# A two-part encoder step on one core: matmul operands at multiples of 512 bytes, small tiles in a pool of their own

## The chip, the cores and the metric

The kernel runs on one core of a Trainium2 chip. The metric is the device time of one execution in microseconds (us), from the first to the last instruction of the core. The kernel before took 1413.92 us (median of three executions: 1413.7, 1413.92 and 1422.26).

The core's engines run side by side and meet at semaphores: PE (matrix multiplications; its weight loads are shown as PEld), DVE (elementwise work, reductions), ACT (elementwise work, exponentials), POOL (elementwise work; it also starts some DMA transfers) and SP (starts most DMA transfers). SBUF is the on-chip memory, PSUM the small one into which PE writes.

## The reference, cut to what matters

All numbers are float32. There are 2048 prompt rows of one stream and 8 x 16 sample rows, which attend to 1024 cached keys each. D is 1024.

```
h = rms_norm(x, norm_g)
z = h @ w_in                                     # 1024 -> 3584 columns
u_a, v_a, g_a, q, k, v, g_b = split(z)           # 7 x 512
# branch A: spatial gate, 4 groups of 128, chunks of 128 positions
vn  = rms_norm(v_a, sgu_norm_g)                  # per group
y_a = u_a * (tril(sgu_w) @ vn + sgu_b) * silu(g_a)
# branch B: differential attention, 4 heads, q and k in two halves of 64
q, k = rms_norm(q, q_norm_g), rms_norm(k, k_norm_g)
s = q.k / 8 - slope_h * |q_pos - k_pos|, block-causal by chunks of 64
o = (softmax(s1) - lam * softmax(s2)) @ v        # lam from four vectors
y_b = rms_norm(o, subln_g) * 0.8 * silu(g_b)     # 0.8 = 1 - lam_init
y = x + concat(y_a, y_b) @ w_out
```

The outputs are y for prompt and sample rows, and the new k, v and v_a. `silu` is computed as 0.5 g (1 + tanh(g/2)), so the tables of `subg` carry the factor 0.5.

## The kernel before, in words

**Arithmetic.** Each float32 operand of a product is split into a high and a low part, both in the fast format `float32r`; `mm3` (L148) then issues three matmuls: high by high, high by low, low by high. A `split` is one ACT copy (the high part) and one subtraction on DVE or POOL (the low part). Most of the 9892 matmuls are such triples: `acc` (projection, 128 x 256), `oo` (output projection, 128 x 512), `oT` (values, 128 x 256). `S` are the scores, and names that end in `_tp` are transposes by the identity `ident`.

**Stages.** There are 17 row tiles of 128 (0 to 15 prompt, 16 the samples). In the profiled execution, whose span is 1410.9 us:

- 0 to about 191 us: the input projection alone (first half of the tiles and the sample rows).
- about 191 to 544 us: the projection woven with the sample attention.
- 544 to about 913 us: the projection of tiles 8 to 15 woven with the prompt attention of query tiles 0 to 7 (four heads, pairs of query tiles); 913 to 942 us: the rest of the projection alone, while the output weights `wo` are loaded and split (L936 to L942).
- 942 to about 1342 us: the output projection woven with the attention of query tiles 8 to 15.
- from about 1342 us: the rest of the output projection with the last values.

**What sets the order.** `weave` (L877) emits two streams of work in turn, by a ratio of their times on PE. When the program is built, a list scheduler then puts the instructions of each engine into one fixed order, by a modelled time line, under the dependencies that tiles and buffers make. On the chip each engine runs its list in that order and only waits for semaphores. In the order of before, the attention of the third stage runs some 1000 emitted instructions behind the place at which `weave` emits it.

**Buffers.** A tile with a tag and `bufs=n` takes the tag's n slots in turn: its first writer waits until the tile that used the slot n allocations earlier has been read for the last time. Two such small tiles matter here:

- `vst` (in `vg_group`, L382 to L403), 2 slots: `va` is copied from the projection's PSUM bank (L392, ACT); ACT squares it and writes sums into `vst` (L400); POOL turns them into factors (L144 to L146); DVE multiplies (`vn`, L403). The PSUM banks of the projection (`acc`, two of them in this stage) come free when `va` and `th` (L367) and their like on ACT and DVE have read them.
- `ost` (in `value_steps`, L629 to L641), 2 slots of its own: the output of a head, `oT`, is copied (`os`, L626), transposed by PE (`o_tp`), squared by ACT with sums into `ost` (L635), POOL makes the factors (L637, L638), and DVE multiplies by the gate (`gbt`, L641).

**Places in memory.** The pools `const`, `const1`, `p1`, `p1g` and `bg` follow each other in SBUF. Small tiles such as `slope` (8 bytes per partition) lie in the same pools as the operands of matmuls, so that the latter start at odd places. By the addresses that the program assigns, modulo 512 bytes: the weights `w` at 448; the transposed rows `xT` of tiles 0 to 3 and 8 to 11 at 128, of tiles 4 to 7 and 12 to 15 at 448, of the samples at 192; `wo` at 480, `yT` at 480 or 192; `kT` and `qT` at 192 or 448; `aT` and `v` of the prompt attention at 128 or 0; `sv` and `saT` of the sample attention at 0.

Of the kernel before, what the change touches and what calls it, by code (L numbers as in the profile page):

```python
# [9 lines left out]
F32 = mybir.dt.float32  # L10
# [3 lines left out]
ALU = mybir.AluOpType  # L14
# [4 lines left out]
P = 128  # L19
# [7 lines left out]
H = 4  # L27
# [5 lines left out]
# buffers  # L33
NEX = (4, 2)        # exponentials of the two softmaxes
NW = 12             # weight chunks
NKB = 6             # chunks of transposed keys
NYT = 2             # halves of a transposed row tile of the output projection
XB = 3              # token tiles on the way in
WB = 5              # weight chunks on the way in, at the start
# what the two streams of a stage get of the tensor engine: the first stream's time over the second's, and how many  # L40
# steps of the second the first may run ahead
RS, AS = 2.8, 100   # projection, sample attention
RA, AA = 2.0, 100   # projection, prompt attention
RB, AB = 0.66, 12   # output projection, prompt attention
RT, AT = 1.8, 0     # output projection, last values
LB = 1.5            # factor on RS for the last sample batch
OB, OT = 9, 6       # time of output projection at the head of its two stages
V0, V1 = 0.25, 1.0  # where in a unit of scores the values of the unit before start and end
QP = 0.3            # and where the queries of the unit after are fetched
CA, CB = "dd", "ad" # engine that scales the second softmax of an even and an odd query tile  # L50
# [7 lines left out]
def trunk_step_kernel(  # L58
# [34 lines left out]

    const = ctx.enter_context(tc.tile_pool(name="const", bufs=1, reuse_waits="tile"))
# [5 lines left out]
    # token tiles: 0..15 prompt, 16 the sample rows  # L100
# [10 lines left out]

    ident = ctile([P, P], "ident")
    mhalf = ctile([P, 8], "mhalf")
    dve.memset(mhalf, -0.5)
    slope = ctile([P, 2], "slope")
    subg = ctile([P, P], "subg")
    neglam = ctile([P, 1], "neglam")

    def constants(lams):
        sp.dma_start(slope, c_slope)  # L120
        sp.dma_start(subg, subln_g[0:1].partition_broadcast(P))
        dve.tensor_scalar_mul(subg, subg, 0.5 * (1.0 - LAM_INIT))
        lame = ctile([P, 2], "lame")
# [34 lines left out]
    def bank(use, name):  # L158
        """The next of the PSUM banks that the stage gives to this use."""
        turn[use] = turn.get(use, -1) + 1  # L160
        b = cur[use][turn[use] % len(cur[use])]
        return psum.tile([P, 512], F32, name=name, tag=f"bank{b}")
# [5 lines left out]
    class Slots:  # L168
        """A pool of equal slots that the streams of a stage share: a tag takes its slots in turn."""
# [17 lines left out]
    def p1_pools(stage, at):  # L187
# [8 lines left out]
        normg = ctile1([P, 8], "normg")  # L196
        qkg = ctile1([P, 2, 2, 64], "qkg")
        sgug = ctile1([P, H, P], "sgug")
        bias_p = ctile1([P, H], "bias_p")
        bias_s = ctile1([P, H], "bias_s")  # L200
        wsT = ctile1([P, 2, H, P], "wsT", F32R)

        def constants1():
            for c in range(2):
                sp.dma_start(qkg[:, 0, c], q_norm_g[0:1].partition_broadcast(P))
                sp.dma_start(qkg[:, 1, c], k_norm_g[0:1].partition_broadcast(P))
# [38 lines left out]
        def xload(t):  # L245
# [9 lines left out]
            st = sb.tile([P, 3], F32, name="xst", tag="xst", bufs=3)  # L255
# [74 lines left out]
        def qk_group(h, tiles, w, loads):  # L330
            for pr, load in zip(pairs(tiles), loads):
# [6 lines left out]
                st = sb.tile([P, 2, 8], F32, name="qst", tag="qst")  # L338
# [7 lines left out]
                pool.tensor_tensor(out=qk[:, :n].rearrange("p n s d -> p n (s d)"),  # L346
                                   in0=z.rearrange("p n s d -> p n (s d)"),
                                   in1=qkg.rearrange("p s c d -> p (s c d)").unsqueeze(1).broadcast_to([P, n, 256]),
                                   op=ALU.mult)
# [32 lines left out]
        def vg_group(h, tiles, w, loads):  # L382
# [5 lines left out]
            for k, (pr, load) in enumerate(zip(pairs(tiles), loads)):  # L388
# [9 lines left out]
                st = sb.tile([P, 2, 2], F32, name="vst", tag="vst")  # L398
# [29 lines left out]
        def stream():  # L428
            """All blocks of columns for the first half of the token tiles and the sample rows, then for the rest."""
# [118 lines left out]
    def score_steps(sl, dist, h, j, ks, qT, wmax, nex, comb, sm):  # L548
        """A step is one chunk of keys for one of the two softmaxes of a query tile."""
        for qi in range(2):  # L550
            t = 2 * j + qi
            w = (t + 1) * P
            st = sl.tile([P, 2, 8], F32, name="sst", tag="sst", bufs=6)
# [38 lines left out]
    def value_steps(sb, vs, h, j, sm):  # L592
# [36 lines left out]
        st = sb.tile([P, 2, 2], F32, name="ost", tag="ost", bufs=2)  # L629
# [17 lines left out]
    def attention(sb, sl, groups, wmax, nk, nv, nex, comb, eng):  # L647
        """A group of pairs of query tiles goes through all heads. The scores of a unit (a pair and a head) run in
        step with the values of the unit before and with the keys and queries of the unit after. Yields None when no
        scores are left."""  # L650
# [28 lines left out]
        for i, (key, j) in enumerate(units):  # L679
            n = size[key[0]]  # L680
            events = []
            # scores
# [5 lines left out]
            # values of the unit before  # L688
# [49 lines left out]
    def sample_scores(sa, b, qkT, qbd, dist_s, res):  # L738
# [8 lines left out]
        st = sa.tile([P, 8], F32, name="sst2", tag="sst2", bufs=2)  # L747
# [56 lines left out]
    def sample_values(sa, b, a):  # L804
# [35 lines left out]
        yield 0  # L840

    def sample_attention(sa):
        """The scores of a batch run in step with the values of the batch before."""
        ss = sample_setup(sa)
        yield pe_time(1024)
        a = None
# [220 lines left out]
```

## Time and profile before

| | before |
|---|---|
| median of three executions | 1413.92 us |
| profiled execution: own time, first to last instruction (span) | 1410.9 us |
| PE busy | 1360.5 us (96%), 9892 matmuls |
| DVE busy | 897.1 us (64%) |
| ACT busy | 794.0 us (56%) |
| POOL busy | 617.6 us (44%) |
| mean granted PE clock | 0.994 |

The profiled execution's own time is its span; nothing is added around it. A line such as L73 is the line of a helper (`mm3`), so groups are told apart by their tiles: `acc<-w,xT` is the projection. A matmul's duration in the records (284 ns for `acc`) is longer than the distance from one start to the next, because matmuls overlap in the array; distances are read from the timeline, where a row gives the time from the first start to the last end of n matmuls in a row.

### The profile page before, as it was taken

To read this page: it belongs to the slowest core of one execution; us is meant where nothing else is said; L and a number is where in the kernel's file an instruction comes from. 1 tells how busy PE (TensorE), PEld (TensorE's weight loads), DVE (VectorE), ACT (ScalarE), POOL (GpSimd) and SP (SyncE) were. 2 spreads that over 40 slices of the span, in tenths; PEclk is the share of its full clock that TensorE was granted. 3 is DMA by queue.
4 is the path that set the end of the run, shared out by engine and by line. 5 is a ranking of instruction groups with operands and counts; after the bars stand their busy time and mean duration, and the time that the engine had idled before them with its cause. 6 is when DMAs were issued, how large, how long until landed. Compare 5 with 4: busy or idle time off the path is not lost.

```text
span 1410.9 us, 27990 instructions
## 1 busy us (share of the span) xinstructions
PE 1360.5 (96%) x9892; PEld 1266.1 (90%) x9892; DVE 897.1 (64%) x2114; ACT 794.0 (56%) x1778; POOL 617.6 (44%) x796
## 2 busy tenths in 40 slices
PE   7999999999999989899999999988999999999998
PEld 6999999999999979899999999986888888888887
DVE  5442366767565764786766767444888778878632
ACT  5442356666655775565554655443777767667520
POOL 2361535555554655656232331243555545444310
PEclk9999999999999999999999999998999999999999
DMA  7533244545444476445343332166555433433223
GB/s 220 175 91 100 78 122 124 169 130 158 130 140 145 142 220 203 112 112 138 96 128 83 99 96 69 42 211 207 149 158 162 142 115 117 143 97 94 75 94 101
DMA packets 209245, 183.06 MB, mean 130 GB/s; under 512 B 21104, under 2 KB 167024, under 8 KB 209104
## 3 DMA queue, kind: packets, MB, share of 16 engines
q1 hardware_dynamic: 199280, 155.17, 36.9%
q0 software_dynamic: 9824, 26.09, 6.8%
q8 instruction: 78, 1.28, 0.4%
q14 instruction: 63, 0.52, 0.1%
HBM read 130.86 MB, written 42.47 MB: 123 GB/s over the span
## 4 chain that ended last, share of the span: by engine, by line
PE 50%; DMA 7%; DVE 5%; ACT 3%; issue 3%; POOL 3%; SPq 1%; ACTq 0%; DVEq 0%; POOLq 0%
PE acc L73 16%; PE oo L73 12%; PE S L73 8%; PE oT L73 7%; PE a_tp L77 4%; DMA wraw<-in_w_in_dram 2%; DMA svraw<-in_cache_v_dram 1%; DMA woraw<-in_w_out_dram 1%; DVE ex L584 1%; DMA x<-in_x_prompt_dram 1%; DVE ex L568 1%; PE y_tp L77 1%; DMA qraw<-q_scr 1%; POOL sv L139 1%; DVE w L306 1%
## 5 line engine op out<-in xcount | busy, mean ns | idle before, releaser
L73 PE MATMUL acc<-w,xT 128*128 128x256 f32 x5376 | 719.4, 284 | 2.5 <-DVE w L306 0.9
L73 PEld LDWEIGHTS acc<-w,xT 128*128 128x128 f32 x5376 | 676.2, 190 | 14.8 <-issue 2.7
L73 PE MATMUL oo<-wo,yT 128*128 128x512 f32 x816 | 223.6, 405 | 6.6 <-ACT yT L138 6.6
L73 PE MATMUL S<-kT,qT 128*128 128x512 f32 (+3 forms) x688 | 185.8, 367 | 6.2 <-DVE sst L568 3.9
L572 ACT ACTIVATE ex<-ex,sst 128x128 f32<-128x128 f32 (+15 forms) x128 | 153.9, 1203 | 61.0 <-DVE sst L568 59.5
L73 PEld LDWEIGHTS oo<-wo,yT 128*128 128x128 f32 x816 | 148.9, 191 | 34.7 <-ACT yT L138 7.6
L306 DVE SCALAR_TENSOR_TENSOR w<-wraw,normg,w 128x256 fp32r<-128x256 f32 x224 | 119.6, 555 | 87.1 <-ACT w L305 79.1
L305 ACT ACTIVATE w<-wraw,normg 128x256 fp32r<-128x256 f32 x220 | 105.8, 505 | 87.8 <-DMA wraw<-in_w_in_dram 75.3
L73 PE MATMUL oT<-aT,v 128*128 128x256 f32 x864 | 151.8, 290 | 2.9 <-ACT aT L138 1.9
L568 DVE CUSTOM_DVE_ANT_0 ex<-S,dist,sst 128x512 f32<-128x512 f32 (+2 forms) x192 | 123.2, 652 | 37.6 <-PE S L73 35.8
L73 PEld LDWEIGHTS oT<-aT,v 128*128 128x128 f32 x864 | 124.3, 189 | 14.5 <-DVE aT L139 3.9
L139 POOL TENSOR_TENSOR sv<-svraw,sv 128x512 fp32r<-128x512 f32 (+1 forms) x72 | 96.6, 1346 | 75.5 <-ACT sv L138 59.1
L73 PEld LDWEIGHTS S<-kT,qT 128*128 128x128 f32 x688 | 110.4, 191 | 21.3 <-DVE sst L568 8.6
L138 ACT CAST aT<-a_tp 128x512 fp32r<-128x512 f32 (+1 forms) x144 | 79.3, 559 | 70.4 <-PE a_tp L77 68.5
L139 DVE TENSOR_TENSOR aT<-a_tp,aT 128x512 fp32r<-128x512 f32 (+1 forms) x144 | 94.3, 658 | 38.2 <-ACT aT L138 37.3
L568 DVE CUSTOM_DVE_ANT_0 ex<-S,dist 128x512 f32<-128x512 f32 (+3 forms) x128 | 79.6, 629 | 29.8 <-PE S L73 16.6
L77 PE MATMUL a_tp<-ident,ex 128*128 128x128 f32 x544 | 83.1, 273 | 4.3 <-DVE ex L584 3.3
L784 POOL TENSOR_TENSOR slo<-slo,dist_s 64x256 f32<-64x256 f32 (+1 forms) x64 | 49.4, 772 | 63.3 <-ACT slo L783 60.5
L139 POOL TENSOR_TENSOR v<-vraw,v 128x512 fp32r<-128x512 f32 x36 | 48.2, 1338 | 54.5 <-ACT v L138 45.4
L77 PEld LDWEIGHTS a_tp<-ident,ex 128*128 128x128 f32 x544 | 63.3, 140 | 8.5 <-DVE gbt L641 1.9
L584 DVE SCALAR_TENSOR_TENSOR ex<-ex,sst 128x1024 f32<-128x1024 f32 (+4 forms) x64 | 65.1, 1038 | 1.1
L588 POOL TENSOR_TENSOR ex<-ex 128x1024 f32<-128x1024 f32 (+4 forms) x32 | 58.4, 1848 | 15.9 <-ACT ex L587 11.4
(144 smaller groups left out, 1925.5 us busy)
## 6 DMA issues: line engine op xcount, KB each, us to landing
wraw<-in_w_in_dram SPq DMA_DIRECT2D x160, 128.0 KB, 2.5
skraw<-in_cache_k_dram SPq DMA_DIRECT2D x64, 256.0 KB, 3.1
svraw<-in_cache_v_dram SPq DMA_DIRECT2D x64, 256.0 KB, 2.9
kT<-k_scr POOLq DMA_DIRECT2D x20, 512.0 KB, 4.6
vraw<-out_dram SPq DMA_DIRECT2D x36, 256.0 KB, 2.8
y<-y_scr SPq DMA_DIRECT2D x34, 256.0 KB, 3.0
out_dram<-xo SPq DMA_DIRECT2D x34, 256.0 KB, 2.1
wraw<-in_w_in_dram SPq DMA_DIRECT2D x128, 64.0 KB, 2.2
```

Source lines behind the costliest of these rows:

```text
L73: pe.last = nc.tensor.matmul(*a, **k).ins
L77: pe.last = nc.tensor.transpose(*a, **k).ins
L138: act.copy(hi, src)
L139: (lo_eng or dve).tensor_tensor(out=lo, in0=src, in1=f(hi), op=ALU.subtract)
L305: act.activation(w[:, 0], r, AF.Copy, scale=normg[:, kc:kc + 1])
L306: dve.scalar_tensor_tensor(out=w[:, 1], in0=r, scalar=normg[:, kc:kc + 1], in1=f(w[:, 0]), op0=ALU.mult, op1=ALU.subtract)
L568: dve.tensor_tensor_reduce(out=ex[c][:, a:b], in0=s, in1=dist[:, off + a:off + b], scale=SLOPES[h], scalar=prev[c], op0=ALU.add, op1=ALU.m ...
L572: act.activation(ex[c][:, :w], ex[c][:, :w], AF.Exp, bias=prev[c], scale=-1.0, accum_out=st[:, c, 6:7])
L584: dve.scalar_tensor_tensor(out=p0, in0=p1, scalar=st[:, 1, 7:8], in1=p0, op0=ALU.mult, op1=ALU.add)
L588: pool.tensor_tensor(out=p0, in0=p1, in1=p0, op=ALU.add)
L784: pool.tensor_tensor(out=lo, in0=lo, in1=dist_s[rh, x:x + w_], op=ALU.add)
```

## The change

1. A new pool `small` at the bottom of SBUF takes all small tiles: the constants as slices of one tile `misc`, and the tags `xst`, `qst`, `sst`, `sst2`, `vst`. `ost` is now allocated under the tag `vst`, so that `vg_group` and `value_steps` take turns in one ring of 3 slots. `sfst` shares `sst2`.
2. The table `qkg` of query and key norms is halved ([P, 2, 64], read twice by a broadcast). Two DMA loads go. The multiplication on POOL (L346), 32 times 128 x 512, becomes two of 128 x 256 each.
3. `subg` moves to `const1`.
4. The pool `bg` is preceded by a pad of 120 columns, and its slots of odd sizes are allocated first. Which slots hold what in the prompt attention of the third stage changes (`qT` in m10 and m0, `eb` in m11).
5. With this, the operands that the front part lists by address all start at multiples of 512 bytes (`w`, `xT`, `wo`, `yT`, `kT`, `qT`, `aT`, `v`, `vhl`, `wsT`, `ident`); only some inputs of transposes and the key slices of the sample scores start elsewhere.

```diff
+    small = ctx.enter_context(tc.tile_pool(name="small", bufs=2, reuse_waits="tile"))
     const = ctx.enter_context(tc.tile_pool(name="const", bufs=1, reuse_waits="tile"))
...
+    misc = small.tile([P, 32], F32, name="misc", tag="misc", bufs=1)
+    mhalf, normg, slope, neglam, lame = [misc[:, a:b] for a, b in ((0, 8), (8, 16), (16, 18), (18, 19), (19, 21))]
+    bias_p, bias_s = misc[:, 21:25], misc[:, 25:29]
+    dve.memset(mhalf, -0.5)
     ident = ctile([P, P], "ident")
-    mhalf = ctile([P, 8], "mhalf")
-    dve.memset(mhalf, -0.5)
-    slope = ctile([P, 2], "slope")
-    subg = ctile([P, P], "subg")
-    neglam = ctile([P, 1], "neglam")
...
-        qkg = ctile1([P, 2, 2, 64], "qkg")
+        subg = ctile1([P, P], "subg")
+        qkg = ctile1([P, 2, 64], "qkg")
...
-            st = sb.tile([P, 3], F32, name="xst", tag="xst", bufs=3)
+            st = small.tile([P, 3], F32, name="xst", tag="xst", bufs=3)
...
-                pool.tensor_tensor(out=qk[:, :n].rearrange("p n s d -> p n (s d)"),
-                                   in0=z.rearrange("p n s d -> p n (s d)"),
-                                   in1=qkg.rearrange("p s c d -> p (s c d)").unsqueeze(1).broadcast_to([P, n, 256]),
-                                   op=ALU.mult)
+                for i in range(n):
+                    pool.tensor_tensor(out=qk[:, i].rearrange("p s (c d) -> p s c d", c=2),
+                                       in0=z[:, i].rearrange("p s (c d) -> p s c d", c=2),
+                                       in1=qkg.unsqueeze(2).broadcast_to([P, 2, 2, 64]), op=ALU.mult)
...
-                st = sb.tile([P, 2, 2], F32, name="vst", tag="vst")
+                st = small.tile([P, 2, 2], F32, name="vst", tag="vst", bufs=3)
...
-            st = sl.tile([P, 2, 8], F32, name="sst", tag="sst", bufs=6)
+            st = small.tile([P, 2, 8], F32, name="sst", tag="sst", bufs=6)
...
-        st = sb.tile([P, 2, 2], F32, name="ost", tag="ost", bufs=2)
+        st = small.tile([P, 2, 2], F32, name="ost", tag="vst", bufs=3)
...
-        st = sa.tile([P, 8], F32, name="sst2", tag="sst2", bufs=2)
+        st = small.tile([P, 8], F32, name="sst2", tag="sst2", bufs=2)
...
+        ctx.enter_context(tc.tile_pool(name="end", bufs=1, reuse_waits="tile", side="right")).tile(
+            [P, 120], F32, name="end", tag="end")
         bg = open_pool(right, "bg")
+        for tag, n in [(m[2], NK), (m[3], NK), (m[7], 1088), (m[11], 1088), ("dist", NK), (r[6], 544)]:
+            bg.tile([P, n], F32, name=tag, tag=tag, bufs=1)
...
-            sa = Slots(bg, kT=m[8:10], qT=m[10:12], ea=[m[7], m[2], m[3]], eb=[m[0]], aT=[m[4], m[1]], v=m[5:7],
+            sa = Slots(bg, kT=m[8:10], qT=[m[10], m[0]], ea=[m[7], m[2], m[3]], eb=[m[11]], aT=[m[4], m[1]], v=m[5:7],
```

The build's order of instructions moves with it, in the third stage alone: PE's list is the same up to its matmul 4345 and again from matmul 7108, the first of the stage after.

The first place is on PE, in the middle of the third stage, after some 5610 matmuls. Before, attention (`oT` values, `a_tp` transposes of the weights of attention, `q_tp` of the queries, `S` scores) lies between stretches of the projection (`acc`, and `mix`, the spatial gate):

```order
L73 MATMUL acc<-w,xT 128x256 x5
L73 MATMUL mix<-vhl,wsT 128x512 x3
L73 MATMUL acc<-w,xT 128x256 x7
L73 MATMUL oT<-aT,v 128x256
L73 MATMUL acc<-w,xT 128x256 x5
L77 MATMUL a_tp<-ident,ex 128x128 x4
L73 MATMUL oT<-aT,v 128x256 x5
L73 MATMUL S<-kT,qT 128x384
L73 MATMUL acc<-w,xT 128x256 x16
```

Now, from the same place on, attention stands alone. These are the first and the last rows of 131 such matmuls between two of the projection:

```order
L73 MATMUL acc<-w,xT 128x256 x4
L73 MATMUL oT<-aT,v 128x256
L77 MATMUL a_tp<-ident,ex 128x128 x4
L73 MATMUL oT<-aT,v 128x256 x5
L73 MATMUL S<-kT,qT 128x384
L73 MATMUL oT<-aT,v 128x256
```

```order
L73 MATMUL oT<-aT,v 128x256
L77 MATMUL a_tp<-ident,ex 128x128 x4
L73 MATMUL oT<-aT,v 128x256 x6
L73 MATMUL acc<-w,xT 128x256 x29
```

After these come 29 of the projection, then 102 matmuls in which attention and a few of the projection take turns; a third run of attention, 72 matmuls without one of the projection, is the last of this attention. It ends at PE's matmul 6362, where before it ended at 7106:

```order
L73 MATMUL oT<-aT,v 128x256 x11
L77 MATMUL o_tp<-ident,os 128x128 x2
L73 MATMUL acc<-w,xT 128x256 x28
L73 MATMUL mix<-vhl,wsT 128x512
L73 MATMUL acc<-w,xT 128x256 x3
L73 MATMUL mix<-vhl,wsT 128x512 x2
L73 MATMUL acc<-w,xT 128x256 x65
```

What was spread over the last 1500 matmuls of the stage now stands in its first half, and some 746 matmuls of the projection follow alone. The splits of `wo` on ACT, DVE and POOL follow the end of this attention in both orders, and so stand earlier too.

The second place is ACT, at the same point of the program. Before, the sums of the spatial gate (`vn,vst`) follow `va` and `th` at once:

```order
L392 COPY va<-acc 128x256
L367 ACTIVATE th<-acc 128x256
L400 ACTIVATE vn,vst<-va 128x128 x2
L498 CAST kT<-k_tp 64x512
L138 CAST aT<-a_tp 128x512
```

Now nearly 60 ACT instructions stand between this `va` and its `vn,vst`, among them the `os,ost` of four units of attention; the next `va`, which frees the projection's bank, comes only after them (lines are those of the changed kernel):

```order
L623 COPY os<-oT 128x256
L632 ACTIVATE os,ost<-o_tp 128x128 x2
L397 ACTIVATE vn,vst<-va 128x128 x2
L569 ACTIVATE ex,sst<-ex,sst 128x896 x2
L136 CAST aT<-a_tp 128x512
L389 COPY va<-acc 128x256
L364 ACTIVATE th<-acc 128x256
```

The `vn,vst` here takes the slot of an `ost` that was allocated three turns earlier in the shared ring, so it stands behind the last reader of that `ost`.

More of the change, by code (lines that the diff above doesn't have):

```diff
@@ L110, in trunk_step_kernel @@
     k_saved = set()
+    misc = small.tile([P, 32], F32, name="misc", tag="misc", bufs=1)
+    mhalf, normg, slope, neglam, lame = [misc[:, a:b] for a, b in ((0, 8), (8, 16), (16, 18), (18, 19), (19, 21))]
+    bias_p, bias_s = misc[:, 21:25], misc[:, 25:29]
+    dve.memset(mhalf, -0.5)
     ident = ctile([P, P], "ident")
-    mhalf = ctile([P, 8], "mhalf")
-    dve.memset(mhalf, -0.5)
-    slope = ctile([P, 2], "slope")
-    subg = ctile([P, P], "subg")
-    neglam = ctile([P, 1], "neglam")
     def constants(lams):
         sp.dma_start(slope, c_slope)
-        sp.dma_start(subg, subln_g[0:1].partition_broadcast(P))
-        dve.tensor_scalar_mul(subg, subg, 0.5 * (1.0 - LAM_INIT))
-        lame = ctile([P, 2], "lame")
         for i, l in enumerate((lambda_q1, lambda_k1, lambda_q2, lambda_k2)):
@@ L194, in ctile1 @@
             return cp.tile(shape, dt, name=name, tag=name)
-        normg = ctile1([P, 8], "normg")
-        qkg = ctile1([P, 2, 2, 64], "qkg")
+        subg = ctile1([P, P], "subg")
+        qkg = ctile1([P, 2, 64], "qkg")
         sgug = ctile1([P, H, P], "sgug")
-        bias_p = ctile1([P, H], "bias_p")
-        bias_s = ctile1([P, H], "bias_s")
         wsT = ctile1([P, 2, H, P], "wsT", F32R)
         def constants1():
-            for c in range(2):
-                sp.dma_start(qkg[:, 0, c], q_norm_g[0:1].partition_broadcast(P))
-                sp.dma_start(qkg[:, 1, c], k_norm_g[0:1].partition_broadcast(P))
+            sp.dma_start(qkg[:, 0], q_norm_g[0:1].partition_broadcast(P))
+            sp.dma_start(qkg[:, 1], k_norm_g[0:1].partition_broadcast(P))
+            sp.dma_start(subg, subln_g[0:1].partition_broadcast(P))
+            dve.tensor_scalar_mul(subg, subg, 0.5 * (1.0 - LAM_INIT))
             sp.dma_start(sgug, sgu_norm_g[0:1].partition_broadcast(P))
@@ L337, in qk_group @@
                 sq = qk.rearrange("p n s (c d) -> p (n s c) d", c=2)[:, :4 * n]
-                st = sb.tile([P, 2, 8], F32, name="qst", tag="qst")
+                st = small.tile([P, 2, 8], F32, name="qst", tag="qst")
                 act.activation(sq.rearrange("p g d -> p (g d)"), z.rearrange("p n s d -> p (n s d)"), AF.Square,
@@ L865, in sample_finish @@
             sp.dma_start(gb[:, h], g_scr[h][T:T + P])
-        st = sa.tile([P, 2, H], F32, name="sfst", tag="sfst", bufs=1)
+        st = small.tile([P, 2, H], F32, name="sfst", tag="sst2", bufs=2)
         junk = sa.tile([P, P], F32, name="sfj", tag="sob")
```

## The prediction

> **What bounds the kernel now.** I read the page first, then the stages as windows, then PE's timeline at the one place where a stage shows PE idle.
>
> ```profile
> span 1410.9 us, 27990 instructions
> ...
> PE 1360.5 (96%) x9892; PEld 1266.1 (90%) x9892; DVE 897.1 (64%) x2114; ACT 794.0 (56%) x1778; POOL 617.6 (44%) x796
> ```
>
> PE is busy 96% of the span and no other engine comes near. So the time can move in two ways only: by the distance between matmuls that follow each other, or by PE waiting. The windows show where PE waits (busy us and count of PE, then of PEld, DVE, ACT and POOL, then PE's clock).
>
> ```profile
> core 0: us, PE busy (x) PEld busy (x) DVE busy (x) ACT busy (x) POOL busy (x), PEclk, DMA share, GB/s
> ...
> 544.00:722.00 178.00, 172.42 (x1393) 168.23 (x1394) 126.53 (x299) 99.62 (x250) 88.88 (x124) 1.00 0.41 114
> 722.00:913.00 191.00, 190.43 (x1549) 187.37 (x1549) 123.22 (x321) 99.45 (x294) 51.15 (x107) 1.00 0.32 89
> 913.00:942.00 29.00, 29.00 (x241) 28.75 (x240) 14.97 (x21) 13.16 (x34) 12.69 (x15) 1.00 0.61 181
> 942.00:1012.00 70.00, 55.96 (x268) 45.00 (x268) 39.51 (x92) 34.36 (x63) 33.46 (x41) 0.90 0.64 192
> ```
>
> The woven third stage (544 to 913 us) is full: after 722 us PE waits 191.00 - 190.43 = 0.57 us in all, at 190.43 / 1549 = 0.123 us a matmul. The start of the fourth stage is the loose place: 70.00 - 55.96 = 14.0 us of waiting, and a granted clock of 0.90. The timeline says why (start, us, row, and in brackets the wait ahead of it).
>
> ```profile
> 942.05 0.60 PE L77 MATMUL y_tp<-ident,y 128*128 128x128 f32 x4
> 947.95 2.07 PE L73 MATMUL oo<-wo,yT 128*128 128x512 f32 x4 [5.31 <-ACT yT L138]
> ...
> 950.53 9.55 PE L73 MATMUL oo<-wo,yT 128*128 128x512 f32 x34
> ...
> 967.90 1.87 PE L73 MATMUL S<-kT,qT 128*128 128x512 f32 x3 [2.07 <-DVE qT L142]
> 969.57 1.48 PE L73 MATMUL oo<-wo,yT 128*128 128x512 f32 x3
> 974.34 0.62 PE L77 MATMUL q_tp<-ident,qraw 128*128 128x128 f32 x2 [3.29 <-DMA qraw<-q_scr]
> 974.61 1.63 PE L73 MATMUL S<-kT,qT 128*128 128x384 f32 x4
> ...
> 980.08 0.86 PE L73 MATMUL oo<-wo,yT 128*128 128x512 f32 x3
> ```
>
> PE waits 5.31 us for a copy on ACT that stands behind the last splits of `wo`, then 2.07 and 3.29 us for queries that were fetched late. Each wait has an echo: the three `oo` at 969.57 take 1.48 us, the same three at 980.08 take 0.86. The clock rows agree:
>
> ```profile
> 945.00:950.00 5.00, 2.05 (x5) 0.71 0.34 110
> 950.00:955.00 5.00, 5.00 (x18) 0.61 1.04 314
> 955.00:960.00 5.00, 5.00 (x24) 1.00 0.94 308
> ...
> 985.00:990.00 5.00, 3.84 (x17) 1.00 0.13 40
> 990.00:995.00 5.00, 3.75 (x24) 1.00 0.77 201
> ```
>
> The clock falls after the long waits and is whole again within 10 us; at 985 to 995 us, where PE idles 2.4 us in single waits of about 1 us, it stays at 1.00.
>
> **The change part by part.**
>
> *The new addresses.* No view shows addresses; those in the text are the program's. `acc` is the largest group (5376 matmuls on prompt tiles), so its pace decides:
>
> ```profile
> L73 PE MATMUL acc<-w,xT 128*128 128x256 f32 x5376 | 719.4, 284 | 2.5 <-DVE w L306 0.9
> ```
>
> A record lasts 0.284 us, far longer than the distance between starts. Windows of the first stage, where the projection streams alone, hold PE only:
>
> ```profile
> 101.00:111.00 10.00, 10.00 (x90) 1.00 0.50 142
> 112.00:122.00 10.00, 10.00 (x86) 1.00 0.18 61
> 178.00:188.00 10.00, 10.00 (x88) 1.00 0.49 136
> ```
>
> So a window of 10 us touches 10.28 us of starts: 10.28 / 90 = 0.114 us from start to start with `xT` at 128 (tiles 0 to 3, 101 to 111 us), 10.28 / 86 = 0.1195 with `xT` at 448 (tiles 4 to 7), and 10.28 / 88 = 0.117 with the very tiles of the first window again, 77 us later. So the address goes with something, but one address has two paces. What both operands at 0 do is shown by `sO`, which lies there already:
>
> ```profile
> 309.59 0.63 PE L73 MATMUL sO<-sv,saT 128*128 128x512 f32 x2
> ```
>
> and, from the view of that tile (shortest, median and longest record in ns),
>
> ```profile
> L73 PE MATMUL sO<-sv,saT x2: 393/395/397, 309.6 to 309.8; 128*128 128x512 f32 x2
> ```
>
> Its second matmul starts 0.63 - 0.395 = 0.235 us after the first. For `oo` at 980.08 it is (0.86 - 0.395) / 2 = 0.233, with `wo` at 480: operands at multiples of 512 bytes are no faster. Bounds for `acc`, from today's mean of some 0.118: all at 0.114 gives 5376 x -0.004 = -22 us, and if `oo` and the rest gain in proportion some -30; all at 0.1195 gives +8. I take **0**, by the row of `sO`, the only one with these addresses.
>
> *The order of the third stage.* The shared ring makes `vn,vst` of the first pair in this half wait for `ost` of units which, in the order of before, ran much later. The projection stops until attention has caught up: 131 matmuls of attention in a row. They take about 131 x 0.123 = 16 us on PE, but each unit goes PE, DVE, ACT, DVE, PE, and DVE has more to do. These are the groups' means over the stage (544 to 942 us; the last columns are busy us and mean ns); the counts by which I multiply are those of DVE's list beside these matmuls.
>
> ```profile
> L306 DVE SCALAR_TENSOR_TENSOR w<-wraw,normg,w 128x256 fp32r<-128x256 f32 x97 | 49.7, 532 | 33.9 <-ACT w L305 33.2
> ...
> L568 DVE CUSTOM_DVE_ANT_0 ex<-S,dist 128x512 f32<-128x512 f32 (+3 forms) x64 | 36.0, 571 | 12.4 <-PE a_tp L77 8.2 <-PE S L73 2.1 <-DMA y_scr<-sfo 0.6
> ...
> L584 DVE SCALAR_TENSOR_TENSOR ex<-ex,sst 128x128 f32<-128x128 f32 (+7 forms) x32 | 28.0, 876 | 0.9
> ...
> L139 DVE TENSOR_TENSOR aT<-a_tp,aT 128x512 fp32r<-128x512 f32 (+1 forms) x40 | 25.4, 635 | 9.7 <-ACT aT L138 9.2
> ...
> L142 DVE SCALAR_TENSOR_TENSOR qT<-q_tp,qT 64x256 fp32r<-64x256 f32 x31 | 13.1, 423 | 3.5 <-ACT qT L141 2.7
> ...
> L641 DVE SCALAR_TENSOR_TENSOR gbt<-o_tp,ost,gbt 128x128 f32<-128x128 f32 x32 | 9.7, 344 | 3.0 <-POOL ost L638 2.9
> ...
> L568 DVE DVE_READ_ACCUMULATOR2_ANT sst<- 128x1 f32 x96 | 8.0, 83 | 0.0
> ```
>
> 17 score chunks with their read-out (17 x 0.654 = 11.1), 6 combinations (5.3), 7 `aT` (4.4), 5 `qT` (2.1), 6 `gbt` (2.1), 3 `w` (1.6): 26.6 us, and with some 20 small ones of one column (reciprocals, scalings) about 28 us on DVE, against 16 on PE. PE loses 28 - 16 = 12 us, less if DVE starts ahead, more with the tail through POOL. The second stretch (102 matmuls, PE 12.5 us, 36 DVE instructions at 28 / 76 = 0.37 each, so 13 us) loses 1 to 3; the third (72 matmuls, the drain of the last units, seven `aT` blocks that each go ACT, DVE, PE) 3 to 6, the gate of the last unit before the bank comes free included. Sum **+18**, from 8 (DVE well ahead) to 30 (each chain exposed). ACT's list behind the waiting `vn,vst` holds the next `va`, `th` and exponentials; for these PE waits. POOL is half idle there.
>
> What is won in exchange in the same stage is nothing that I can see: after 722 us PE had lost only 0.57 us. The 746 matmuls that follow alone stream as at 913 to 942 us (29.00 of 29.00 busy).
>
> The clock during the catch-up: PE waits there in pieces of under 1 us, as at 985 to 995 us, so I expect 1.00. [...]
>
> *The fourth stage's start.* `wo` is split earlier now, so ACT, DVE and POOL are free when the projection ends. Two rows on POOL show the queue that goes:
>
> ```profile
> 946.49 1.26 POOL L139 TENSOR_TENSOR wo<-woraw,wo 128x512 fp32r<-128x512 f32 x1 [2.85 <-ACT wo L138]
> 947.69 0.85 POOL L485 DMA_DIRECT2D kraw<-out_dram  x1
> ```
>
> The loads of keys and queries, behind that split in POOL's list, can go earlier, until the buffers bind. Of the 5.31 us some 1.8 stay (copy and subtraction of `yT`): -3.5. With that wait goes its echo: 34 `oo` took 9.55 us where 33 x 0.233 + 0.4 = 8.1 would do, and the four ahead 2.07 for 1.1, so -2.4. Half of 2.07 + 3.29 and of its echo, (1.48 - 0.86) at 969.57 and about as much twice more: -2.7 and -1.0. Sum **-10**, between 0 (the copy is late for another reason: the load of `y`) and -15 (all of it). What is late next is `S` waiting on DVE, as at 985 us.
>
> *The rest*, at nothing. POOL's multiplication in two:
>
> ```profile
> L346 POOL TENSOR_TENSOR qk<-z,qkg 128x512 f32<-128x512 f32 x16 | 21.3, 1331 | 3.8 <-DVE z L344 2.5 <-PE oT L73 0.9
> ...
> L394 POOL TENSOR_TENSOR gb<-sg,subg 128x256 f32<-128x256 f32 x16 | 12.2, 764 | 0.9
> ```
>
> 2 x 0.764 - 1.331 = +0.2 us each, 32 times 0.2 is 6.4 us on an engine at 44%; behind it come only the stores of q and k, so PE doesn't see it (if it did, +6.4). Two loads fewer on SP and the other slots of `bg` move no instruction on PE.
>
> **Sum:** 1410.9 + 0 + 18 - 10 = 1418.9 for a span like the profiled one. The median of the runs is 3.0 us above that span (1413.92), so **1422**. Two runs of three lie within 0.2 us and the third 8 above; 1% (14 us) is about what can be told from no change, so the bounds are 1400 and 1428. The forecast's own range, with its terms' ends, is 1406 to 1434.
>
> **The rivals.**
>
> *Aligned operands are faster.* For it: tiles 0 to 3 at 128 had 0.114 for 10 us, tiles at 448 never. Against it: `sO` at 0 and the same tiles at 0.117. If all `acc` went at 0.114, -22 to -30, and the order costs +8 net: 1414 + 8 - 26 = **1396**. It decides from about 4 ns a matmul: 8 + 14 = 22 us over 5376. Chance 0.25.
>
> *The catch-up is dearer, and drops the clock.* The projection waits on one long chain at its end: `o_tp`, ACT's squares, POOL's factors, `gbt`, then `vn,vst` and `va`, all in a row. If PE idles there for 3 us or more, the echo is that of 947.95, 2.4 us, each of three times: +7. With the stretches at their upper 30 and -10 at the start: 1414 + 30 + 7 - 10 = **1441**. For it: every unit of attention is such a chain, and no `acc` is left to fill it. Against it: the waits are short by the DVE sum. It decides above 2 us for a single wait. Chance 0.30.
>
> *The early split pays more than the catch-up costs*: DVE is ahead when the catch-up begins (+8) and all of the start's waits go (-15): 1414 - 7 = **1407**. Within 1%. Chance 0.10. *The order is as before on the chip*, since the ring never binds: excluded, as the order is fixed in the build.
>
> **How the numbers follow.** Forecast 0.35, dearer catch-up 0.30, faster operands 0.25, early split 0.10. Of the forecast's cases a fifth end above 1428; of the dearer catch-up's, 0.24 of 0.30; of the faster operands', 0.20 lie under 1400, with 0.03 of the early split. So faster 0.23, within 1% 0.46, slower 0.31. The range that leaves out about a tenth on each side runs from 1393 (0.10 of the operands' rival lies below) to 1444 (0.10 of the dearer catch-up above).
>
> **What would show it.** In the changed trace: windows of 10 us of `acc` alone with 87 or 88 matmuls (90 or more: the operands' rival); a stretch near 730 us of some 28 us with PE under 70% busy and rows of `S` and `a_tp` that wait for DVE; PE's clock in it (below 1.00: the clock's rival); the last `o_tp` of this attention near 850 us; and the wait ahead of the first `oo` under 2.5 us. If that stretch is full, the term of the order is wrong.

## The result, and the profile after

The changed kernel takes 1467.07 us (median of five executions, 1462.93 to 1471.28) against 1417.3 us before (five executions, 1413.7 to 1422.26). The ratio is 1.0356 with a 95% interval of 1.0331 to 1.0381: 3.6% slower, some 50 us. The forecast was 1422 us, and no case of it reached so far.

The profiled execution has a span of 1460.9 us against 1410.9, so its difference, 50.0 us, can be read stage by stage. Its time on record is 1462.93 us, 2.0 us more than its span. So what stands ahead of the prediction, that nothing is added around the span, is not right: in the records of all runs it is 1.7 to 2.1 us, in both kernels. The page first:

```profile
span 1460.9 us, 28072 instructions
...
PE 1386.8 (95%) x9892; PEld 1285.2 (88%) x9892; DVE 895.0 (61%) x2114; ACT 796.2 (55%) x1778; POOL 623.6 (43%) x828
```

The work of DVE and ACT is what it was, within 3 us. PE shows 26 us more of busy time for the same 9892 matmuls, and the rest of the 50 us is idle. The windows of the third stage and of the stage's end (busy us and counts of PE, PEld, DVE, ACT and POOL, PE's clock, then the transfers) say where:

```profile
554.00:730.00 176.00, 172.75 (x1393) 169.49 (x1393) 122.40 (x296) 98.78 (x243) 90.02 (x135) 1.00 0.41 116
730.00:875.00 145.00, 119.38 (x808) 105.83 (x806) 93.43 (x249) 74.72 (x215) 39.37 (x88) 0.92 0.28 79
875.00:910.00 35.00, 27.64 (x191) 27.21 (x192) 21.33 (x32) 14.59 (x36) 16.06 (x17) 0.85 0.47 132
910.00:1006.00 96.00, 95.91 (x788) 95.18 (x788) 30.04 (x69) 27.67 (x85) 16.99 (x30) 1.00 0.31 92
```

Until 730 us the stage runs as before (172.75 us of 176 busy). From 730 to 910 us PE idles 33 us at a lowered clock. From 910 us the projection streams alone. Smaller windows, cut near the rows of PE's timeline where attention stands without the projection, give each catch-up its price; the two rows below them are the first and the one behind the last of the first 131 matmuls:

```profile
738.10:774.50 36.40, 24.70 (x124) 17.58 (x123) 28.91 (x79) 23.02 (x65) 12.66 (x29) 0.91 0.34 90
774.50:778.00 3.50, 3.50 (x31) 3.50 (x31) 2.48 (x5) 0.58 (x1) 1.41 (x3) 1.00 0.00 0
778.00:795.00 17.00, 13.04 (x75) 11.11 (x74) 12.86 (x36) 11.51 (x36) 6.41 (x14) 0.80 0.36 113
850.30:877.90 27.60, 14.77 (x75) 11.17 (x73) 13.03 (x32) 12.38 (x38) 5.16 (x14) 0.79 0.20 56
...
736.92 0.28 PE L73 MATMUL oT<-aT,v 128*128 128x256 f32 x1
...
774.49 3.64 PE L73 MATMUL acc<-w,xT 128*128 128x256 f32 x29
```

The first lasts 37.6 us, from 736.9 to 774.5; its 131 matmuls at the stage's 0.123 us would be 16.1: 21.5 us lost. Then come 29 matmuls of the projection without a wait. The second stretch, the 102 matmuls behind these, lasts 20.5 us (12.5 at the same pace): 8 us lost, all before 795 us. The third lasts 27.6 us for 72 matmuls (8.9): 19 us lost. Its rows, with the wait ahead of each in brackets, show the chain that was named and never priced link by link:

```profile
858.53 0.44 PE L77 MATMUL o_tp<-ident,os 128*128 128x128 f32 x2 [1.91 <-ACT os L623]
861.52 1.11 PE L77 MATMUL a_tp<-ident,ex 128*128 128x128 f32 x4 [2.56 <-DVE gbt L638]
863.31 0.58 PE L73 MATMUL oT<-aT,v 128*128 128x256 f32 x1 [0.68 <-ACT aT L136]
...
872.33 0.45 PE L77 MATMUL o_tp<-ident,os 128*128 128x128 f32 x2 [0.46 <-ACT os L623]
877.86 5.95 PE L73 MATMUL acc<-w,xT 128*128 128x256 f32 x28 [5.08 <-DVE sg L366]
...
903.58 8.68 PE L73 MATMUL acc<-w,xT 128*128 128x256 f32 x58 [4.50 <-DVE usg L375]
```

The last `o_tp` of this attention stands at 872.33 us, and the projection starts again after 5.08 us, when `sg` has read its bank: ACT's squares, POOL's factors, `gbt`, `vn`, `va`, `th` and `sg` come one after another. The four transposes at 861.52 us take 1.11 us where four took 0.60 elsewhere: the clock is down (0.52 from 860 to 870 us). A part of these losses is the clock's. From 730 to 910 us the clock column (0.92 over 145 us, 0.85 over 35) means some 34 us at half speed, in which the records show PE busy for 26.5 us. If that work took half as long at full clock (the transposes took 0.60 in place of 1.11 us), the clock's part is at most some 13 us, an estimate. A fourth loss was not foreseen at all: at 899 us the projection waits 4.50 us for `usg`, which stands on DVE behind the splits of `wo`. These now lie among the projection's work and are paced by the transfer of the weights:

```profile
900.60 1.14 ACT L136 CAST wo<-woraw 128x512 fp32r<-128x512 f32 x2 [2.04 <-DMA woraw<-in_w_out_dram]
...
901.64 0.38 ACT L364 ACTIVATE th<-acc 128x256 f32<-128x256 f32 x1
901.77 1.33 DVE L137 TENSOR_TENSOR wo<-woraw,wo 128x512 fp32r<-128x512 f32 x1 [1.77 <-ACT wo L136]
903.03 0.41 DVE L375 SCALAR_TENSOR_TENSOR usg<-sg,acc 128x256 f32<-128x256 f32 x1
```

21.5 + 8 + 19 + 4.5 = 53 us. The third stage, from the first `S` (543.41 us before, 552.91 now) to the first `y_tp` (942.05 before, 1006.15 now), is 453.2 us long in place of 398.6: 54.6 us more. So nearly all of it is in these four places. The stages before add 9.5 us. The fourth stage gives back 14.1 (1410.9 - 942.05 = 468.9 before, 1460.9 - 1006.15 = 454.8 now): the wait ahead of its first `oo` has shrunk from 5.31 to 0.77 us. The first `S` of before, then the rows of the changed kernel:

```profile
543.41 0.22 PE L73 MATMUL S<-kT,qT 128*128 128x128 f32 x1
...
552.91 0.23 PE L73 MATMUL S<-kT,qT 128*128 128x128 f32 x1
...
1006.15 0.60 PE L77 MATMUL y_tp<-ident,y 128*128 128x128 f32 x4
1007.52 1.19 PE L73 MATMUL oo<-wo,yT 128*128 128x512 f32 x4 [0.77 <-ACT yT L136]
...
1008.90 8.00 PE L73 MATMUL oo<-wo,yT 128*128 128x512 f32 x34
```

And the pace of the projection alone, the same three windows as in the prediction, now with all operands at multiples of 512 bytes:

```profile
101.00:111.00 10.00, 10.00 (x86) 1.00 0.32 81
112.00:122.00 10.00, 10.00 (x86) 1.00 0.53 157
178.00:188.00 10.00, 10.00 (x86) 1.00 0.32 88
```

86 matmuls in each: the slow pace of before (0.1195 us) everywhere. The count of 90 that tiles 0 to 3 once had is gone.

### The profile page after: what moved, and what is told of

The parts are those of the page before. It is cut to its first block, busy times and chain, and to the rows that moved or that the text cites. A ratio compares the mean times of both kernels' runs of the same rounds, so it can differ in the third digit from the quotient of the medians.

```text
span 1460.9 us, 28072 instructions
## 1 busy us (share of the span) xinstructions
PE 1386.8 (95%) x9892; PEld 1285.2 (88%) x9892; DVE 895.0 (61%) x2114; ACT 796.2 (55%) x1778; POOL 623.6 (43%) x828
## 5 line engine op out<-in xcount | busy, mean ns | idle before, releaser
L73 PEld LDWEIGHTS acc<-w,xT 128*128 128x128 f32 x5376 | 686.2, 194 | 22.4 <-issue 7.1
L73 PE MATMUL oo<-wo,yT 128*128 128x512 f32 x816 | 218.5, 399 | 2.1 <-ACT yT L136 2.1
L303 DVE SCALAR_TENSOR_TENSOR w<-wraw,misc,w 128x256 fp32r<-128x256 f32 x224 | 117.6, 547 | 90.8 <-ACT w L302 81.0
L73 PE MATMUL oT<-aT,v 128*128 128x256 f32 x864 | 155.4, 296 | 9.1 <-ACT aT L136 7.0
L302 ACT ACTIVATE w<-wraw,misc 128x256 fp32r<-128x256 f32 x220 | 105.6, 505 | 84.2 <-DMA wraw<-in_w_in_dram 66.9
L73 PEld LDWEIGHTS S<-kT,qT 128*128 128x128 f32 x688 | 110.4, 192 | 28.5 <-DVE sst L565 16.1
L77 PE MATMUL a_tp<-ident,ex 128*128 128x128 f32 x544 | 86.6, 281 | 9.9 <-DVE gbt L638 5.5
```

What stands on the lines that cost most here:

```text
L73: pe.last = nc.tensor.matmul(*a, **k).ins
L77: pe.last = nc.tensor.transpose(*a, **k).ins
L302: act.activation(w[:, 0], r, AF.Copy, scale=normg[:, kc:kc + 1])
L303: dve.scalar_tensor_tensor(out=w[:, 1], in0=r, scalar=normg[:, kc:kc + 1], in1=f(w[:, 0]), op0=ALU.mult, op1=ALU.subtract)
```

## The experiments

Two theories stood against each other. **A:** the common tag of `vst` and `ost` costs nearly all, by the order. **B:** the new addresses cost most of it. A third question came with the paces: which addresses make a matmul fast.

**Own slots for both tiles** (run e1_own_rings). The changed kernel with `vst` in two slots of its own, which lie in the unused pad at the top of memory, and `ost` in two; no operand moves.

```diff
-                st = small.tile([P, 2, 2], F32, name="vst", tag="vst", bufs=3)
+                st = ends[0].tile([P, 2, 2], F32, name="vst", tag="vst", bufs=2)
...
-        st = small.tile([P, 2, 2], F32, name="ost", tag="vst", bufs=3)
+        st = small.tile([P, 2, 2], F32, name="ost", tag="ost", bufs=2)
```

> The changed kernel with one thing undone: vst and ost have two slots each of their own again; every matmul operand stays at a multiple of 512 bytes. Theory A (the shared tag costs nearly all): the order of the third stage is that of before, the catch-up stretches vanish, and what is left is the pace of the projection, 120 ns in place of a mean near 118 (5376 x 2 = 11 us at most), and the start: 1417 + 5 to 14, so 1420 to 1432, ratio 1.003 to 1.01. Theory B (the new addresses cost most of the 50 us): 1450 to 1465, ratio 1.025 or more. Rival C (aligned operands gain something that the catch-up hides): below 1405.

Measured: 1417.33 us against 1414.97 before, ratio 1.0015 (0.9999 to 1.003): as theory A said, even a little under its lower end of 1420. Theory B falls. PE's order differs from that of before only between its matmuls 4345 and 4957, so the rest of the change, which the prediction said moves nothing on PE, moves a little there. The windows of this kernel (PE's busy us and count, clock) are full where the changed kernel's were not:

```profile
554.00:730.00 176.00, 173.09 (x1397) 1.00 0.42 118
730.00:875.00 145.00, 144.29 (x1164) 1.00 0.36 98
875.00:910.00 35.00, 35.00 (x286) 1.00 0.20 56
```

Everything in the change but the common tag, the addresses and the divided multiplication on POOL included, costs between nothing and 0.3% in all.

**The common tag alone** (run e2_ring_in_before). The kernel before, with `vst` and the third stage's `ost` in one tag of three slots. Pads keep the prompt's projection at the offsets that it had; of the rest, both operands of a pair keep theirs or move by the same 32 or 96 bytes, but for the samples' rows and the last four tiles of the output projection.

```diff
-                st = sb.tile([P, 2, 2], F32, name="vst", tag="vst")
+                st = ring[0].tile([P, 2, 2], F32, name="vst", tag="vst", bufs=3)
...
-        st = sb.tile([P, 2, 2], F32, name="ost", tag="ost", bufs=2)
+            st = ring[0].tile([P, 2, 2], F32, name="ost", tag="vst", bufs=3)     # third stage
```

> The kernel before with one thing added: in the third stage vst and ost share one tag of three slots, as in the changed kernel; the addresses of projection, scores and values keep their phases of before. Theory A: the whole loss of the third stage is here, 1417 + 35 to 48, so 1452 to 1465, ratio 1.025 to 1.034. Theory B: within 10 us of before, ratio under 1.007.

Measured: 1464.43 us, ratio 1.0342 (1.0323 to 1.0361): the whole loss, on the old addresses. PE's order has the same 131 and 72 matmuls of attention without the projection, at the same places. The waits of PE from 720 to 915 us (us in total, times, longest) are those of the changed kernel:

```profile
PE acc L73 <- DVE usg L379: 6.6, 1, 6.6
PE oT L73 <- ACT aT L139: 6.5, 8, 1.4
PE acc L73 <- DVE sg L370: 5.1, 1, 5.1
PE a_tp L77 <- DVE gbt L647: 5.0, 4, 2.6
```

In the changed kernel they read 4.5, 5.7, 5.1 and 5.0 us. Theory A holds, from both sides.

**More slots in the common tag** (run e3_ring8). Eight in place of three, addresses unchanged.

```diff
-                st = small.tile([P, 2, 2], F32, name="vst", tag="vst", bufs=3)
+                st = ends[0].tile([P, 2, 2], F32, name="vst", tag="vst", bufs=8)
...
-        st = small.tile([P, 2, 2], F32, name="ost", tag="vst", bufs=3)
+        st = ends[0].tile([P, 2, 2], F32, name="ost", tag="vst", bufs=8)
```

> The changed kernel with eight slots in the shared tag in place of three, addresses unchanged. If the number of slots is what binds (a slot is still being read when it is wanted again), the catch-up goes and the time is that of own slots, 1420 to 1432. If the shared tag binds by its order (the tiles of one tag are taken in the order in which the program allocates them, however many slots there are), the order on PE still has 131 attention matmuls in a row and the time stays within 10 us of the changed kernel: 1457 to 1477.

Measured: 1467.51 us, ratio 1.0362 (1.0345 to 1.0379), as with three. So it is not a slot that is still being read, and the reason given ahead of the prediction, a slot of three turns earlier, is not what binds. In the build, ACT's list has `vn,vst` again right behind the `os,ost` that was allocated just before it, and PE's list again 131 matmuls of attention in a row; the window shows PE as idle as in the changed kernel (119.38 there):

```profile
730.00:875.00 145.00, 121.96 (x804) 0.89 0.28 79
```

The tiles of one tag are taken in the order of their allocation, and the list is fixed by that order, whatever is free.

**The same bytes under two tags** (run e9_two_and_one). Two slots for `vst`, one for `ost`: the three slots of the changed kernel, divided.

```diff
-                st = small.tile([P, 2, 2], F32, name="vst", tag="vst", bufs=3)
+                st = small.tile([P, 2, 2], F32, name="vst", tag="vst", bufs=2)
...
-        st = small.tile([P, 2, 2], F32, name="ost", tag="vst", bufs=3)
+        st = small.tile([P, 2, 2], F32, name="ost", tag="ost", bufs=1)
```

> The changed kernel with the same three small slots under two tags: two for vst, one for ost; no address of an operand moves and no byte more is used. If it is the common tag that costs, and not that a slot is missing, the time is that of the run with own slots: 1413 to 1421, ratio 0.998 to 1.005. If the values of one unit now wait for the factors of the unit before (one slot for ost), attention is late and some 5 to 15 us are lost: 1422 to 1432.

Measured: 1417.4 us against 1411.95 before in this comparison, ratio 1.0028 (1.0009 to 1.0046): that of own slots, and the window is full.

```profile
730.00:875.00 145.00, 144.95 (x1170) 1.00 0.36 101
```

The common tag saved no memory that two tags would have needed: `ost` does with a single slot.

**Moving the operands against each other** (run e4_phase). In before, `xT` at 128 with `w` at 448 (192 behind it, modulo 512) had two paces, 0.114 and 0.117 us; `xT` at 448 (0 behind) had 0.1195 always; the samples' rows at 192 (256 behind) too. In the changed kernel all are 0 behind, and all are slow. That suggested the distance between the two, not the multiple of 512. All kernels from here on have own slots.

```diff
                 w = sb.tile([P, 2, 256], F32R, name="w", tag="w", bufs=NW)
+                if not wpad:
+                    wpad.append(sb.tile([P, 16], F32, name="wpad", tag="wpad", bufs=1))
...
         sbg = stage.enter_context(tc.tile_pool(name="p1g", bufs=2, reuse_waits="tile"))
+        sbg.tile([P, 32], F32, name="pad1g", tag="pad1g", bufs=1)
```

> Own slots as in the first of these runs, and the transposed rows xT moved against the weights w, which stay at a multiple of 512 bytes: tiles 4 to 7 and 12 to 15 by 64 bytes, tiles 0 to 3 and 8 to 11 by 192, the sample rows by 416. Theory P (what matters is the distance of the two operands, and 64 more than a multiple of 128 is better than 0): acc runs at 113 or 118 ns on both sets of tiles, mean near 117 in place of 120, 5376 x 3 = 16 us under the run with own slots, 1404 to 1416. If only the distance of 192 modulo 512 is good, one set keeps 120 and half of it is won: 8 us. If the distance does nothing: the same time as with own slots.

Measured: 1407.7 us, ratio 0.9941 (0.9924 to 0.9958), a little less than before, within the range of theory P. The operands of scores, values and output projection move too, but both of a pair by the same bytes, the last four tiles of the output projection excepted. Windows of the projection alone, PE's rows:

```profile
101.00:111.00 10.00, 10.00 (x90) 1.00 0.49 133
112.00:122.00 10.00, 10.00 (x90) 1.00 0.35 113
...
163.00:173.00 10.00, 10.00 (x90) 1.00 0.25 71
178.00:188.00 10.00, 10.00 (x88) 1.00 0.49 129
```

**All tiles 64 bytes behind** (run e5_all64).

```diff
-        sbg.tile([P, 32], F32, name="pad1g", tag="pad1g", bufs=1)
...
+        endp.tile([P, 88], F32, name="end", tag="end")     # brings the samples' rows to 64 as well
```

> As the run e4_phase, with xT of all tiles and of the sample rows 64 bytes behind w modulo 512 (there one half was 192 behind and went at 113 or 118 ns, the half at 64 mostly at 113). Theory P (a distance of 64 is the good one): both halves at 113 when they stream alone, 2500 matmuls gain 3 ns each, 7 us under e4_phase: 1398 to 1403, ratio 0.987 to 0.991, faster than both kernels. If the two halves only share something that gives one of them the fast pace, or the place in memory beyond 512 bytes decides: no gain over e4_phase, 1405 to 1410.

Measured: 1403.88 us against 1415.01, ratio 0.9926 (0.9909 to 0.9944): the fastest of all, though the gain over e4_phase is at most half of the 7 us expected (3.8 by the medians, 2 by the ratios), and the two intervals overlap, so a gain over e4_phase is not shown.

**The same in the fourth stage** (run e6_stage4), with the stationary operand 64 bytes ahead in place of behind, since memory allowed only that:

```diff
+        ypool.tile([P, 16], F32, name="ypad", tag="ypad", bufs=1)
...
+                sb.tile([P, 16], F32, name="apad", tag="apad", bufs=1)
...
+            sb.tile([P, 16], F32, name="kpad", tag="kpad", bufs=1)
```

> The projection as in e5_all64 (the sample rows at 416), and in the fourth stage the stationary operand 64 bytes below the moving one (448 modulo 512) for scores, values and the first 13 tiles of the output projection. If a distance of 448 is as good as 64 for these shapes, values go from 118 to 113 ns (624 x 5 = 3 us) and the 512-wide ones (scores, output projection; 230 to 234 ns) gain some 3 ns (1100 x 3 = 3 us), hidden in part by the waits on DVE: 2 to 6 us under e5_all64. If the distance matters for the projection alone: the same within 2 us.

Measured: 1408.38 us, ratio 0.9967 (0.9951 to 0.9984): no gain, and some 4 us less good than e5_all64. In the records the values still start some 118 ns apart and the output projection some 231 (118.3 and 231.3 in the kernel before), so in this run the distance did nothing that shows for these shapes. Of the 4.2 us between the two profiled spans (1401.1 and 1405.3), 2.6 are there when the fourth stage begins (first `y_tp` at 933.84 and 936.48 us). The samples' rows, the sole difference in the projection's addresses, account for an estimated 336 matmuls x 5 ns = 1.7 us of them (a distance of 416 bytes against 64 in the table below: 119.9 against 114.2 ns alone, 119.4 against 115.6 woven); the rest stays open.

**Two more distances, and the kernel before shifted** (runs e7_other_distances, one execution of 1409.71 us, and e8_before_shift, one of 1415.85 us).

```diff
+                    wpad.append(sb.tile([P, 32], F32, name="wpad", tag="wpad", bufs=1))     # e7: 128 behind
...
+        sbg.tile([P, 48], F32, name="pad1g", tag="pad1g", bufs=1)                            # e7: 320 behind
...
+                    wpad.append(sb.tile([P, 16], F32, name="wpad", tag="wpad", bufs=1))     # e8, in the kernel before
```

> One look at two more distances of xT from w: 128 (tiles 4 to 7, 12 to 15) and 320 (tiles 0 to 3, 8 to 11). Seen so far: 0 and 256 give 120 ns, 64 gives 113, 192 gives 113 or 118. If odd multiples of 64 are good and even ones are not: 128 gives 120, and 320 gives 113 or 118. If the distance must be under 128: both 120. Time by the first: 1409 to 1415.

> The kernel before with 64 bytes left free behind w, nothing else: w stays at 448, xT of tiles 4 to 7 and 12 to 15 comes to 0 (distance 64 for 0 before), xT of tiles 0 to 3 and 8 to 11 to 192 (distance 256 for 192 before). If the distance decides and not the multiple of 512: the first set goes from 120 to 113, the second from 113 or 118 to 120, together 2688 x (3 - 6) = 8 us less, some 1407. If multiples of 512 decide: the first set may gain, and the second stays at its 117.

e7_other_distances came as expected in time; 128 took 118.6 ns, not quite 120. e8_before_shift did not come down to the 1407 that was expected: its set at 64 ran at 118 ns in the lone stretch, not 113, and its other set lost what 192 had given before. One execution of each says little of the time; the paces are another matter. The records of these traces, matched with the program's addresses, give the distance from one start to the next of two `acc` that follow each other (mean over all such pairs below 160 ns; "alone" is 52 to 188 us, "woven" the rest):

| `xT` behind `w`, modulo 512 | `w` at | kernel | alone, ns | woven, ns |
|---|---|---|---|---|
| 0 | 448 | before | 120.0 | 119.2 |
| 0 | 0 | changed | 120.0 | 119.4 |
| 256 | 448 | e8 | 119.9 | 119.3 |
| 128 | 0 | e7 | 118.6 | 118.7 |
| 416 (samples' rows) | 0 | e4 | 119.9 | 119.4 |
| 192 | 448 | before | 115.5 | 117.3 |
| 192 | 0 | e4 | 115.3 | 117.4 |
| 320 | 0 | e7 | 114.2 | 115.4 |
| 64 | 0 | e5 | 114.2 | 115.6 |
| 64 | 448 | e8 | 117.7 | 115.6 |

The three distances that are odd multiples of 64 bytes are below the others in every kernel; the even ones and 416 stay between 118.6 and 120. `w` at 448 did as `w` at 0, the two places tried, at distance 0 (120.0 ns alone in both) and at 192 (115.5 and 115.3), and at 64 in the woven part (115.6 in both), though not alone (117.7 and 114.2): the multiple of 512 is not what sets the rows apart. Nor does the place of `xT` by itself decide: at 0 it belongs to the slow rows with `w` at 0 (120.0) and to the quicker with `w` at 448 (117.7), and at 192 it is the other way round (115.3 and 119.9). The odd distances showed two paces, 113 and 118 ns, and stayed with one for many microseconds (at 192 in the kernel before 113.3 from 100.6 to 108 us, 117.8 from 177 to 187); what sets it I did not find, and e8_before_shift, which had the slower of the two over nearly the whole lone stretch and the quicker for more than half of the woven one, at the same places, shows that the place alone doesn't.

## Why the prediction was wrong

**The order of the third stage: right mechanism, mis-sized by a factor of three.** The step that failed is the sum "+18, from 8 to 30"; the trace has 53 us in its place. Term by term:

- First stretch: +12 forecast, 21.5 measured. The work on DVE was forecast well (28 us; the window has 28.91), but the stretch lasted 37.6 us. I priced it as if DVE, the busiest engine, were busy throughout. No engine was (the window of 36.40 us has PE busy for 24.70, ACT for 23.02, POOL for 12.66): each unit's chain goes round PE, ACT, DVE and POOL, and without the projection between there is nothing to do in the gaps. The bound "each chain exposed" should have been the value, since the order shows attention alone; and even the upper end of the sum, 30 us, was too low.
- Third stretch: 3 to 6 forecast, 19 measured. I counted seven `aT` blocks, not the links around them: 1.91 for `os`, 2.56 for `gbt`, 5.08 from the last `o_tp` to the freed bank, the latter through seven instructions on three engines.
- Second stretch: 1 to 3 forecast, 8 measured, for the same reason.
- 4.5 us for `usg` behind the splits of `wo`: not forecast. I asked what the earlier splits give to the fourth stage, and not whom they stand in front of.

Of the signs named beforehand, the long stretch near 730 us with PE busy for 68% of it, the clock below 1.00 and the short wait ahead of the first `oo` all came; the last `o_tp` came at 872.33 us, not near 850.

**The clock.** "PE waits there in pieces of under 1 us", from which 1.00 was expected, was wrong twice. The waits were longer (1.79, 1.45, 2.56, 5.08 us), and the clock fell already after the first of these, at 750.08 us:

```profile
749.45 0.62 PE L73 MATMUL S<-kT,qT 128*128 128x384 f32 x2 [1.79 <-DVE sst L565]
751.53 0.90 PE L77 MATMUL a_tp<-ident,ex 128*128 128x128 f32 x3 [1.45 <-DVE gbt L638]
```

with the clock windows

```profile
740.00:750.00 10.00, 6.42 (x37) 1.00 0.48 131
750.00:760.00 10.00, 7.56 (x32) 0.66 0.38 99
...
746.67:750.08 3.41, 1.58 (x6) 1.00 0.27 80
750.08:756.91 6.83, 5.19 (x22) 0.50 0.53 138
...
860.00:870.00 10.00, 7.39 (x31) 0.52 0.05 15
```

This is the rival "the catch-up is dearer, and drops the clock", which had a chance of 0.30. Its mechanism is what happened; its price, 1441 us, was too low, since it took the stretches at the upper 30 and three echoes at 7, 37 in all, where 53 were due. Its condition, a single wait of 2 to 3 us, was too strict.

**The fourth stage's start: right.** Forecast -10, from 0 to -15; measured -14.1 for the whole stage, the first wait down to 0.77 us (forecast: under 2.5). In e1_own_rings, where `wo` is split as late as before, the stage is 465.6 us long (1415.3 - 949.70), 3.3 less than before without the earlier splits; some 11 are left for these.

**The addresses: 0 was forecast, with +8 as the upper bound.** The projection's pace went to the upper bound, 120.0 ns alone, 119.4 woven. In the kernel with own slots this and all the rest of the change cost 0 to 0.3%. POOL's divided multiplication cost POOL 6.0 us (617.6 to 623.6; 6.4 forecast) and PE nothing that shows. The row of `sO` from which I took the value was no good witness: it has 512 columns, where starts lay 0.235 us apart at 0 and 0.233 with `wo` at 480, while the pace of the projection's 256 went from 114.2 to 120.0 ns with the distance. The rival "aligned operands are faster" read the right clue, 90 against 86 matmuls in 10 us, and named the wrong cause: it was 192 bytes between the two operands that went with the 90, and the change took it away.

**The stages before the third: 0 forecast, 9.5 us measured.** The smaller part is the pace: the kernel with own slots, at the same pace and in the same order, has 85 to 86 matmuls in 10 us of the lone projection. The larger part, some 6 us, is the start. The first 50 us, before and now:

```profile
0.00:50.00 50.00, 39.69 (x301) 38.02 (x302) 27.11 (x84) 27.20 (x54) 11.66 (x29) 1.00 0.71 220
...
0.00:50.00 50.00, 36.29 (x249) 35.23 (x250) 25.06 (x76) 25.81 (x49) 11.58 (x29) 0.90 0.70 208
```

52 matmuls fewer at 0.12 us are 6.2 us. In the changed kernel the split of `xT` waits on DVE behind a product for lambda, whose inputs arrive late, and PE waits 3.6 us for it. The kernels e1_own_rings and e4_phase, which keep that part of the change, had 265 and 272, so this varies, and what the moved loads of `subg` and `qkg` have to do with it was not tried: that cause stays open.

**The range.** The forecast's own range, "with its terms' ends" 1406 to 1434, does not come out of the terms: the order (8 to 30) and the start (0 to -15) alone give 1407 to 1444. The result lies beyond both.

## What to carry to other kernels

Two streams that run at different distances behind their emission must not share a buffer tag, however many slots it has: the tiles of a tag are taken in the order of allocation, and the stream ahead is tied to the one behind. When an order shows a stream of short dependent steps without the work that filled its gaps, price it by the latency of one round through all engines times the rounds, not by the busiest engine's sum, and add the drop of PE's clock (an estimated 13 us at most here, where the clock was 0.92 and 0.85). When a pace differs between groups of the same shape, test the relation of the two operands' addresses before the alignment of each.

## What the runs showed of the hardware that I had not expected

For the projection's matmuls (256 float32r columns, each with its own weight load), the start-to-start distance went by how far the stationary operand lies behind the moving one, modulo 512: alone, 119.9 to 120.0 ns at 0 and 256 bytes, 118.6 at 128, and 114.2 to 117.7 at 64, 192 and 320; 0, 64 and 192 were measured with the moving operand at either of two places, 0 and 448. The values, of 256 columns too, stayed at some 118 ns at 448 in e6_stage4, an odd multiple that the projection did not have. Over 5376 matmuls this is worth some 13 us (e5_all64 at 1403.88 us, e1_own_rings at 1417.33, each beside runs of the kernel before at 1415.0), and the kernel with it beats both. With 512 columns no difference beyond some 3 ns was seen (the output projection 231.3 ns before and 229.8 in the changed kernel, `sO` 232.9 and 233.5).

In the first stretch PE's clock fell to half at 750.08 us, after waits of which none was longer than 1.79 us: in the 3.41 us ahead PE was busy for 1.58. In all eleven traces the recorded changes of the granted clock lie whole multiples of 3.41 us apart, so the steps between can be counted by PE's busy share. Of the 52 steps at full clock with PE busy for less than half, 51 were followed by half speed; of the 4126 with more than 55%, 8 were. In the traces of the kernel before and of the changed kernel alone, from the first record of the clock on (15.26 and 12.80 us), it was 11 of 11 (4 and 7, PE busy for at most 0.49 of the step), and none of 797.
